# Half-row matmuls for the gates of a recurrent branch, two channel tiles to a group

## The chip, the cores and the metric

The kernel runs on one core of one Trainium2 chip. The time is device microseconds of one execution of the whole kernel. Besides plain timed runs there is one profiled execution, whose trace shows every engine's instructions: PE (TensorE's matmuls), PEld (its weight loads), DVE (VectorE), ACT (ScalarE), POOL (GpSimd) and SP (the engine that issues most DMAs). Data lies in a memory of 128 partitions; matmul results go to PSUM, which has eight banks of 128 partitions by 512 float32.

## The reference

One decoder block on 512 tokens of 1024 channels: a mixer with a pooling branch and a recurrent branch, then a gated convolutional FFN and a gated input embedding. The change is in the recurrent branch:

```python
xc = causal_dwconv(xb, conv_w, conv_b)                     # 512 tokens x 1024 channels
xh = xc.reshape(b, s, RNN_HEADS, RNN_HEAD_DIM)             # 16 heads of 64 channels
gates = jnp.einsum('bshi,ghij->gbshj', xh, w_gates)        # two gates, 64x64 weights per head
gates = gates.reshape(2, b, s, RNN_WIDTH) + b_gates[:, None, None, :]
r = sigmoid(gates[0]); i = sigmoid(gates[1])
log_a = -LRU_C * r * softplus(-lru_lambda)
u = sqrt(-expm1(2.0 * log_a)) * i * xc                     # 1 in place of the root at token 0
h = scan(h_t = exp(log_a_t) * h_{t-1} + u_t)
y_rnn = (h * gelu(gb)) @ w_rg_out
```

Each head's gate values depend on that head's 64 channels alone.

## The kernel before

Everything is kept with channels on partitions and the 512 tokens along the free dimension; 128 channels are a channel tile, and a channel tile of the recurrent branch holds two heads. Float32 products are made of three matmuls (`mm3`, L169 to L173): both operands are split into a high part, rounded to the type that TensorE takes at full rate (cast by ScalarE, `hi`), and the rest (subtracted by VectorE, `lo`), and high x high, high x low and low x high are summed in one bank.

The order on TensorE is the order in which the code is written; the other engines are ordered by a scheduler, with chains of their own for the sigmoids and other functions on ScalarE (`act`, L137) and for the recurrent branch's work on VectorE (`inv`). Weights are loaded by DMAs in SP's queue, split, and kept some tiles ahead in six buffers each.

The stage around the change is the loop `for n in range(12)` (L537). Four input tiles of the recurrent branch (`rx`) are made before it. Each step multiplies one more input tile (`in_tile(n)`, 24 matmuls), and for the branch's channel tiles goes through:

- `evac` (L454): VectorE scales the bank of an input tile into memory; tiles 8 and up of this count go to the GeLU gate's buffers `rg_t`.
- `conv_first`, `conv_rest`, `conv_low` (L472 to L487): the causal convolution, giving `xc`, and its high and low parts `xcs`, the gate matmuls' moving operand.
- `gates(c)`, at n = c + 4: six matmuls, three into each of two banks, one bank for gate r and one for gate i. The weights are block diagonal 128x128 tiles in `bdh` and `bdl`: head 2c's 64x64 block stands in the upper rows and left columns, head 2c+1's in the lower rows and right columns, and zeros (two POOL memsets, L397 and L398) elsewhere. Two sigmoids on ScalarE, 128 partitions each, follow.
- `gated(c)`, one step later (L503): VectorE multiplies gate i with `xc`.

After the loop `rnn_decay` (L505) makes the decay and runs the scan on VectorE, `rnn_out` multiplies with the GeLU gate, and `rnn_split` splits the result for the output product much later. Meanwhile TensorE goes on with the merge gates' and the pooling branch's input tiles (`IN_ORDER`); `pool_map` (from 170 us on) multiplies the pooled groups, which VectorE makes after the scan.

Of the kernel before, what the change touches and what calls it, by code (L numbers as in the profile page):

```python
# [8 lines left out]
F32 = mybir.dt.float32  # L9
F32R = mybir.dt.float32r  # L10
AF = mybir.ActivationFunctionType
ALU = mybir.AluOpType

P = 128
S = 512
D = 1024
KD = D // P
# [3 lines left out]
EPS = 1e-6  # L21
WINDOWS = (2, 4, 8, 16)
PAD = 16
AHEAD = 4
AHEAD0 = 2
LAG = 4
# [26 lines left out]
C_BG = 48  # L53
# [12 lines left out]
def block_kernel(  # L66
# [20 lines left out]
    nc = tc.nc  # L87
    ACT, V, PE = nc.scalar, nc.vector, nc.tensor

    const = ctx.enter_context(tc.tile_pool(name="const", bufs=1))  # L90
# [15 lines left out]
    def nm(s):  # L106
        uid[0] += 1
        return f"{s}{uid[0]}"

    def bank():  # L110
        return psum.tile([P, S], F32, tag="ps", name=nm("ps"))

    def temp(dt=F32, n=S):
        return tmp.tile([P, n], dt, tag="t", name=nm("t"))

    def slot(dt=F32):
        return mid.tile([P, S], dt, tag="m", name=nm("m"))

    def quad(tag, dt=F32R):
        return big.tile([P, 4, S], dt, tag=tag, name=nm(tag))  # L120
# [4 lines left out]
    def behind(ins, name):  # L125
        tc.add_manual_dep(
            ins.ins,
            name,
            mybir.DependencyInfo(mybir.DependencyClass.NoSync, mybir.DependencyReason.DATA),
            reason="order on the engine",  # L130
        )
# [3 lines left out]
    def act(o, i, func, after=None, **kw):  # L135

        ins = ACT.activation(o, i, func, **kw)  # L137
        after = after or last_func[0]
        if after is not None:
            behind(ins, after)  # L140
        last_func[0] = ins.ins.name
        return ins
# [3 lines left out]
    def inv(ins):  # L146

        if last_v[0] is not None:
            behind(ins, last_v[0])
        last_v[0] = ins.ins.name  # L150
        return ins
# [9 lines left out]
    def sub(o, a, b):  # L161
        V.tensor_tensor(o, a, b, ALU.subtract)  # L162

    def split(hi, lo, src):

        last_copy[0] = ACT.copy(hi, src)  # L166
        sub(lo, src, hi.bitcast(F32))

    def mm3(o, a, b, start, stop, **kw):  # L169
        (ah, al), (bh, bl) = a, b  # L170
        PE.matmul(o, ah, bh, start=start, stop=False, **kw)  # L171
        PE.matmul(o, ah, bl, start=False, stop=False, **kw)  # L172
        PE.matmul(o, al, bh, start=False, stop=stop, **kw)  # L173


    col = const.tile([P, C_END], F32, tag="col", name="col")
# [14 lines left out]
    def c1(j):  # L191
        return col[:, j : j + 1]
# [122 lines left out]

    def weight(key, ahead=AHEAD):
        i = order.index(key)
        while nxt[0] <= min(i + ahead, len(order) - 1):
            prep(order[nxt[0]])
            nxt[0] += 1  # L320
        return ready[key]
# [24 lines left out]
    def ht(k):  # L346
        return hth[k // 4][:, k % 4, :], htl[k // 4][:, k % 4, :]
# [3 lines left out]
    for k in range(KD):  # L351
        raw = xraw[k]
# [4 lines left out]
        hi, lo = ht(k)  # L357
        ht_done = ACT.activation(hi, raw, AF.Identity, scale=c1(C_GMIX + k)).ins.name
        V.scalar_tensor_tensor(lo, raw, c1(C_GMIX + k), hi.bitcast(F32), ALU.mult, ALU.subtract)
        if k % 2 == 1 and k < 7:  # L360
            if k > 1:
                xt = quad("C", F32)
                a = k // 2 - 1
# [23 lines left out]
    for k in range(KD):  # L387
        w = weight(("rx", k // 2), ahead=3)
        (wh, wl), (hh, hl) = w, ht(k)
        for i, (a, b) in enumerate(((wh, hh), (wl, hh), (wh, hl))):  # L390
            for m in range(4):
                o = (k % 2) * S + m * P
                PE.matmul(rx[m], a[:, o : o + P], b, start=k == 0 and i == 0, stop=k == KD - 1 and i == 2)  # L393


    bdh, bdl = quad("C"), quad("C")
    nc.gpsimd.memset(bdh.bitcast(F32), 0.0)  # L397
    nc.gpsimd.memset(bdl.bitcast(F32), 0.0)  # L398
    raw = wpool.tile([P, D], F32, tag="raw", name=nm("raw"), bufs=6)
    nc.sync.dma_start(raw, w_bd)  # L400
    H = P // 2
    for q in range(2):
        pr = slice(q * H, (q + 1) * H)
        hi, lo = (
            b.rearrange("p a (c j) -> p (a c) j", j=P)[pr, :, q * H : (q + 1) * H] for b in (bdh, bdl)
        )
        split(hi, lo, raw[pr].rearrange("p (c j) -> p c j", j=H))


    lam = col[:, C_LAM : C_LAM + 8]  # L410
# [1 line left out]
    mabs, e, f, s, s2, ncol, n2col = sp  # L412
# [31 lines left out]
    def in_tile(m):  # L444
        w = weight(("in", m), ahead=AHEAD if m > 6 else AHEAD0)
        ps = bank()
        for k in range(KD):
            mm3(ps, pick(w, k * P, (k + 1) * P), ht(k), k == 0, k == KD - 1)
            if m == 0 and k == 0:
                spread_rstd()  # L450
        return ps

    def scaled(ps, o):
        return V.tensor_tensor(o, ps, rb, ALU.mult)  # L454

    xs, xc, xcs, sig = {}, {}, {}, {}
    r_t, a_t, rg_t = {}, {}, {}
    rgq = [quad("C", F32), quad("C", F32)]

    def evac(n, ps):  # L460
        if n < 8:
            with urgent():
                xs[n] = temp()
                inv(scaled(ps, xs[n]))
        else:
            c = n - 8
            rg_t[c] = rgq[c // 4][:, c % 4, :]
            inv(scaled(ps, rg_t[c]))

    def conv_first(c):  # L470
        xc[c] = slot()
        ina(ACT.activation(xc[c], xs[c], AF.Identity, scale=c1(C_CONVW + 24 + c), bias=c1(C_CONVB + c)))  # L472

    def conv_rest(c):
        a = xc[c]
        for d in (1, 2, 3):
            inv(
                V.scalar_tensor_tensor(
                    a[:, d:], xs[c][:, : S - d], c1(C_CONVW + (3 - d) * 8 + c), a[:, d:], ALU.mult, ALU.add
                )  # L480
            )
        xcs[c] = slot(F32R), slot(F32R)
        ina(ACT.copy(xcs[c][0], a))

    def conv_low(c):
        hi, lo = xcs[c]
        inv(V.tensor_tensor(lo, xc[c], hi.bitcast(F32), ALU.subtract))  # L487

    def gates(c):
        pss = []  # L490
        for g in range(2):
            ps = bank()
            o = (c % 4) * P
            w = bdh[:, 2 * g + c // 4, o : o + P], bdl[:, 2 * g + c // 4, o : o + P]
            mm3(ps, w, xcs[c], True, True)
            pss.append(ps)
        r_t[c] = slot()
        act(r_t[c], pss[0], AF.Sigmoid, bias=c1(C_BG + c))
        sig[c] = temp()
        act(sig[c], pss[1], AF.Sigmoid, bias=c1(C_BG + 8 + c))  # L500

    def gated(c):
        inv(V.tensor_tensor(xc[c], sig[c], xc[c], ALU.mult))  # L503
# [33 lines left out]
    for n in range(12):  # L537
        banks.append(in_tile(n))
        if n == 0:
            for c in range(4):  # L540
                evac(c, banks[c])
            conv_first(0)
        if n < 8:
            if n < 7:
                if n + 1 in xs:
                    conv_first(n + 1)
            conv_rest(n)
        if 0 < n <= 8:
            conv_low(n - 1)
        if 0 <= n - LAG <= 7:  # L550
            gates(n - LAG)
        if 0 <= n - LAG - 1 <= 7:
            gated(n - LAG - 1)
        evac(4 + n, banks[4 + n])
        if n < 7 and n + 1 not in xc:
            conv_first(n + 1)
# [7 lines left out]
    def pool_tile(g):  # L564
        w = WINDOWS[g]
        ps = in_tile(12 + g)
        u = temp(n=S + PAD)
        V.memset(u[:, :PAD], 0.0)
        with tc.high_priority(offset=300):
            scaled(ps, u[:, PAD:])  # L570
        acc, d = u, 1
        while d < w:
            nx = temp(n=S + PAD)
            o = 2 * d if 2 * d < w else PAD
            V.tensor_tensor(nx[:, o:], acc[:, o:], acc[:, o - d : S + PAD - d], ALU.add)
            acc, d = nx, 2 * d
# [62 lines left out]
    for m in range(KD):  # L639
        w = weight(("wpo", m))  # L640
# [3 lines left out]
        w = weight(("wrg", m))  # L644
# [4 lines left out]
        a, b = gate[m], gate[8 + m]  # L649
# [4 lines left out]
        if m == PLE_AT:  # L654
            pled = dram.tile([S, D], F32, name="pled")
            pq = []
            for k in range(2):
                raw = temp()
# [8 lines left out]
    def token_major(name, nkp, lhs, tail=3):  # L667
# [10 lines left out]
        for t in range(NT):  # L678
            for kp in range(nkp - tail, nkp):
                for h in range(2):  # L680
                    w = weight((name, kp, h), ahead=AHEAD if t else 1)
                    for kk in range(2):
# [58 lines left out]
    def h2(b, c):  # L741

        return tuple(v[c][:, :, b * HALF : (b + 1) * HALF] for v in (h2h, h2l))

    def products(o, w, i, form, start):
        for k in range(4):
            lhs = tuple(v[:, i, k * P : (k + 1) * P] for v in w)
            rhs = tuple(v[:, k, :] for v in form)
            mm3(o, lhs, rhs, start and k == 0, k == 3, skip_group_check=True)

    def up_plain(f, b):
        for i in range(2):
            d = gb if f % 10 == 1 else ub
            if f < 20 and b == 0:
                d[i] = bank()
            w = weight(("up", 0, f), ahead=AHEAD - PLAIN.index(f) if b == 0 else AHEAD)
            products(d[i][:, b * HALF : (b + 1) * HALF], w, i, h2(b, f // 10 - 1), f < 20 and b == 0)
# [30 lines left out]
    for f in (5, 6, 7, 3):  # L788
        q = big.tile([P, 2, 4, HALF], F32R, tag="A", name=nm("A"))
# [141 lines left out]
    for t, i, pair in token_major("wd", 12, hid_split):  # L931
# [5 lines left out]
        with urgent():  # L937
            add_norm(pair, g_fpost, res)
            for h in range(2):
                n = slot()  # L940
# [7 lines left out]
    for h in range(2):  # L948
        for t in range(NT):
            i = 2 * (t % 2) + h  # L950
            o = temp()
            parts = ((0, S // 2), (S // 2, S)) if (h, t) == (1, NT - 1) else ((0, S),)
            for a, b in parts:
                ps = bank()
                for k in range(KD):
                    w = weight(("wpg", k // 2, h))
                    q = (k % 4) * P
# [85 lines left out]
```

## Time and profile before

| | |
|---|---|
| time, three runs | 769.15, 769.66, 769.69 us (median 769.66) |
| profiled execution | 769.33 us, its span 767.5 us |
| granted TensorE clock | 0.999 |
| PE busy | 761.7 us |
| DVE busy | 525.0 us |
| ACT busy | 395.1 us |
| gate matmuls | 48, the first at 56.4 us, the last at 105.1 us |
| sigmoids of the gates | 16 |

The span runs from the first to the last instruction; the profiled execution's own time is 1.8 us longer. In the timeline a row has its start, its length, the engine, the line of the kernel, the operation, the tile written and the tiles read, and the shape. A matmul's recorded length covers its passage through the array, so that records overlap: what one costs in a full stream is the distance from start to start. Of a waiting engine the trace says what ended its wait.

### The profile page before, as it was taken

The page shows a single profiled execution, that of the slowest core. Times are in us where ns is not written, and L with a number is a line of the kernel's source. Part 1 is how long each engine was busy: PE and PEld are TensorE (multiplying, and loading weights), DVE is VectorE, ACT ScalarE, POOL GpSimd, SP SyncE. Part 2 cuts the span into 40 slices and gives each one's busy share as a digit, 9 for nine tenths or more (in the row PEclk, how much of TensorE's full clock was granted, in tenths as well). Part 3 has the DMA queues.
Part 4 walks back from the last instruction along what each step waited for, and adds up shares of the span by engine and source line. Part 5 has one row for each costly group of instructions (what it writes and reads, how often), then busy time and mean ns, then how long its engine had stood idle before and what let it go on. Part 6 is the DMA issues. An engine that isn't in the chain of part 4 may idle for free.

```text
span 767.5 us, 11024 instructions
## 1 busy us (share of the span) xinstructions
PE 761.7 (99%) x4377; PEld 674.6 (88%) x4377; DVE 525.0 (68%) x710; ACT 395.1 (51%) x627; POOL 18.6 (2%) x29
## 2 busy tenths in 40 slices
PE   9999999999999999999999999999999999999997
PEld 7888888888888888889999999999999888888886
DVE  4898446998354655589998888889978332335852
ACT  6845369735232342277866666666685322224631
POOL 2000000000000000010000000000000000001100
PEclk9999999999999999999999999999999999999999
DMA  9752211233324449312233333333368323320111
GB/s 331 283 186 83 82 69 56 62 117 110 123 80 141 138 136 328 110 71 84 95 124 99 107 111 110 111 110 111 110 207 313 139 88 105 102 90 1 56 56 55
DMA packets 42004, 93.87 MB, mean 122 GB/s; under 512 B 3297, under 2 KB 3937, under 8 KB 41953
## 3 DMA queue, kind: packets, MB, share of 16 engines
q1 hardware_dynamic: 41808, 93.07, 35.9%
q8 instruction: 34, 0.56, 0.3%
q14 instruction: 18, 0.14, 0.1%
q10 hardware_dynamic: 144, 0.10, 0.0%
HBM read 86.87 MB, written 6.29 MB: 121 GB/s over the span
## 4 chain that ended last, share of the span: by engine, by line
PE 96%; DMA 2%; SPq 0%; DVE 0%; ACT 0%; POOL 0%; issue 0%; DVEq 0%
PE ps L171 32%; PE ps L172 32%; PE ps L173 32%; DMA C<-in_x_dram 1%; PE ps L700 1%; PE ps L393 1%; DMA col<-in_cols_dram 0%; ACT C L378 0%; SPq L356 0%; DVE lo L162 0%; POOL s L329 0%; PE ps L440 0%; SPq L364 0%; SPq L303 0%; DVE t L384 0%
## 5 line engine op out<-in xcount | busy, mean ns | idle before, releaser
L162 DVE TENSOR_TENSOR lo<-raw,hi 128x1024 fp32r<-128x1024 f32 (+2 forms) x167 | 193.4, 1178 | 88.0 <-ACT hi L311 66.7
L171 PE MATMUL ps<-A,hi 128*128 128x256 f32 (+1 forms) x608 | 199.5, 328 | 0.0
L173 PE MATMUL ps<-A,lo 128*128 128x256 f32 (+1 forms) x608 | 199.4, 328 | 0.0
L172 PE MATMUL ps<-A,hi 128*128 128x256 f32 (+1 forms) x608 | 199.4, 328 | 0.0
L311 ACT CAST hi<-raw 128x1024 fp32r<-128x1024 f32 (+1 forms) x94 | 94.1, 1008 | 154.2 <-PE ps L172 74.0
L173 PEld LDWEIGHTS ps<-A,lo 128*128 128x128 f32 x608 | 114.6, 188 | 10.1
L172 PEld LDWEIGHTS ps<-A,hi 128*128 128x128 f32 x608 | 114.6, 188 | 9.9
L171 PEld LDWEIGHTS ps<-A,hi 128*128 128x128 f32 x608 | 114.6, 188 | 9.9
L171 PE MATMUL ps<-C,hi 128*128 128x256 f32 (+1 forms) x392 | 118.0, 301 | 0.0
L172 PE MATMUL ps<-C,hi 128*128 128x256 f32 (+1 forms) x392 | 117.9, 301 | 0.0
L173 PE MATMUL ps<-C,lo 128*128 128x256 f32 (+1 forms) x392 | 117.8, 301 | 0.0
L171 PE MATMUL ps<-hi,A 128*128 128x512 f32 x256 | 100.0, 391 | 0.0
L173 PE MATMUL ps<-hi,A 128*128 128x512 f32 x256 | 99.7, 389 | 0.0
L172 PE MATMUL ps<-lo,A 128*128 128x512 f32 x256 | 99.7, 389 | 0.0
L166 ACT CAST hi<-raw 128x1024 fp32r<-128x1024 f32 x70 | 72.5, 1052 | 35.1 <-PE ps L172 24.6
L172 PEld LDWEIGHTS ps<-C,hi 128*128 128x128 f32 x392 | 74.2, 189 | 2.6
L171 PEld LDWEIGHTS ps<-C,hi 128*128 128x128 f32 x392 | 74.2, 189 | 2.5
L173 PEld LDWEIGHTS ps<-C,lo 128*128 128x128 f32 x392 | 74.2, 189 | 2.5
L173 PEld LDWEIGHTS ps<-hi,A 128*128 128x128 f32 x256 | 48.1, 188 | 10.0
L171 PEld LDWEIGHTS ps<-hi,A 128*128 128x128 f32 x256 | 48.1, 188 | 9.9
L172 PEld LDWEIGHTS ps<-lo,A 128*128 128x128 f32 x256 | 48.1, 188 | 9.7
L162 DVE TENSOR_TENSOR A<-m,A 128x512 fp32r<-128x512 f32 x40 | 26.0, 686 | 14.6 <-ACT A L166 14.2
(148 smaller groups left out, 918.5 us busy)
## 6 DMA issues: line engine op xcount, KB each, us to landing
raw<-in_w_up_dram SPq DMA_DIRECT2D x48, 512.0 KB, 3.4
raw<-in_w_in_dram SPq DMA_DIRECT2D x32, 512.0 KB, 3.8
raw<-in_w_down_dram SPq DMA_DIRECT2D x24, 512.0 KB, 3.4
raw<-in_w_rg_out_dram SPq DMA_DIRECT2D x8, 512.0 KB, 3.3
raw<-in_w_o_dram SPq DMA_DIRECT2D x8, 512.0 KB, 3.4
raw<-in_w_ple_gate_dram SPq DMA_DIRECT2D x8, 512.0 KB, 3.4
m<-in_rows_dram SPq DMA_DIRECT2D x10, 256.0 KB, 5.7
m<-in_x_t_dram SPq DMA_DIRECT2D x8, 256.0 KB, 7.3
```

The lines of the kernel that those rows point to most:

```text
L162: V.tensor_tensor(o, a, b, ALU.subtract)
L166: last_copy[0] = ACT.copy(hi, src)
L171: PE.matmul(o, ah, bh, start=start, stop=False, **kw)
L172: PE.matmul(o, ah, bl, start=False, stop=False, **kw)
L173: PE.matmul(o, al, bh, start=False, stop=stop, **kw)
L311: ACT.copy(hi, raw)
L393: PE.matmul(rx[m], a[:, o : o + P], b, start=k == 0 and i == 0, stop=k == KD - 1 and i == 2)
L700: PE.transpose(ps[:, q * P : (q + 1) * P], a[:, q * P : (q + 1) * P], ident)
```

## The change

The block diagonal tiles go. The gate weights now stand in one buffer `bd`: for channel tile c, 128 columns, of which the first 64 are gate r's weights and the last 64 gate i's, on rows 0 to 63 for head 2c and on rows 64 to 127 for head 2c+1, with the high parts in one half of the buffer and the low parts in the other. A gate matmul takes 64 rows of weights and 64 rows of `xcs` and writes 128 partitions of a bank of its own: partitions 0 to 63 are the head's gate r, 64 to 127 its gate i. The two heads of a channel tile use the two halves of TensorE's rows, in turn, and two banks.

Two channel tiles make a group of 12 matmuls with four banks: the groups stand behind input tiles 5, 7, 9 and 11, where before the six matmuls of one channel tile stood behind each of the input tiles 4 to 11. Since a bank now holds r and i of one head, four sigmoids of 64 partitions take the place of two of 128 for each channel tile; two of the four write to the other half of the partitions than they read, and take their bias from a small tile `bias` that two DMAs in SP's queue fill from the DRAM columns. The first channel tile's `gated` comes right behind its group, the second one's a step later. The two POOL memsets go, and one split of 128 partitions takes the place of two of 64.

```diff
-    bdh, bdl = quad("C"), quad("C")
-    nc.gpsimd.memset(bdh.bitcast(F32), 0.0)
-    nc.gpsimd.memset(bdl.bitcast(F32), 0.0)
+    bd = quad("C").rearrange("p (s a) c -> p s (a c)", s=2)
     raw = wpool.tile([P, D], F32, tag="raw", name=nm("raw"), bufs=6)
     nc.sync.dma_start(raw, w_bd)
-    H = P // 2
-    for q in range(2):
-        pr = slice(q * H, (q + 1) * H)
-        hi, lo = (
-            b.rearrange("p a (c j) -> p (a c) j", j=P)[pr, :, q * H : (q + 1) * H] for b in (bdh, bdl)
-        )
-        split(hi, lo, raw[pr].rearrange("p (c j) -> p c j", j=H))
+    split(
+        *(bd[:, i].rearrange("p (c g j) -> p g c j", g=2, j=HEAD) for i in range(2)),
+        raw.rearrange("p (g c j) -> p g c j", g=2, j=HEAD),
+    )
+    bias = const.tile([P, KD], F32, tag="bias", name="bias")
+    nc.sync.dma_start(bias[:HEAD], cols[HEAD:, C_BG : C_BG + KD])
+    nc.sync.dma_start(bias[HEAD:], cols[:HEAD, C_BG + KD : C_BG + 2 * KD])
...
-    def gates(c):
-        pss = []
-        for g in range(2):
-            ps = bank()
-            o = (c % 4) * P
-            w = bdh[:, 2 * g + c // 4, o : o + P], bdl[:, 2 * g + c // 4, o : o + P]
-            mm3(ps, w, xcs[c], True, True)
-            pss.append(ps)
-        r_t[c] = slot()
-        act(r_t[c], pss[0], AF.Sigmoid, bias=c1(C_BG + c))
-        sig[c] = temp()
-        act(sig[c], pss[1], AF.Sigmoid, bias=c1(C_BG + 8 + c))
+    def gates(cs):
+        pss = {}
+        for c in cs:
+            pss[c] = bank(), bank()
+            hi, lo = xcs[c]
+            o = slice(c * P, (c + 1) * P)
+            for i, (a, b) in enumerate(((0, hi), (0, lo), (1, hi))):
+                for ps, pr in zip(pss[c], HEADS):
+                    PE.matmul(ps, bd[pr, a, o], b[pr], start=i == 0, stop=i == 2)
+        ba, bb = HEADS
+        for c in cs:
+            r_t[c] = slot()
+            sig[c] = temp()
+            g = C_BG + c
+            act(r_t[c][ba], pss[c][0][ba], AF.Sigmoid, bias=col[ba, g : g + 1])
+            act(sig[c][ba], pss[c][0][bb], AF.Sigmoid, bias=bias[bb, c : c + 1])
+            act(r_t[c][bb], pss[c][1][ba], AF.Sigmoid, bias=bias[ba, c : c + 1])
+            act(sig[c][bb], pss[c][1][bb], AF.Sigmoid, bias=col[bb, g + KD : g + KD + 1])
...
-        if 0 <= n - LAG <= 7:
-            gates(n - LAG)
-        if 0 <= n - LAG - 1 <= 7:
+        if n > LAG and (n - LAG) % 2:
+            gates((n - LAG - 1, n - LAG))
+            gated(n - LAG - 1)
+        elif n > LAG:
             gated(n - LAG - 1)
```

`HEADS` are the row slices 0 to 63 and 64 to 127. The names and lines of the changed kernel stand some lines lower: `mm3` at L171 to L175, `act` at L139, the gate matmuls at L500.

More of the change, by code (lines that the diff above doesn't have):

```diff
@@ L23 @@
 PAD = 16
+HEAD = P // 2
+HEADS = slice(0, HEAD), slice(HEAD, P)
 AHEAD = 4
```

## The prediction

> **What bounds the kernel now.** I began with the page's busy shares and the chain of waits.
>
> ```profile
> span 767.5 us, 11024 instructions
> PE 761.7 (99%) x4377; PEld 674.6 (88%) x4377; DVE 525.0 (68%) x710; ACT 395.1 (51%) x627; POOL 18.6 (2%) x29
> ...
> PE 96%; DMA 2%; SPq 0%; DVE 0%; ACT 0%; POOL 0%; issue 0%; DVEq 0%
> ```
>
> TensorE is busy for 761.7 of 767.5 us and makes up 96% of the chain. Only a stage table tells whether that holds where the gates are, so I cut the span at the first and after the last gate matmul (stages 56.30 to 105.30) and at the first pool map (170). The columns are the length, then PE, PEld, DVE, ACT and POOL busy, the granted clock, the DMA share and GB/s.
>
> ```profile
> 56.30:105.30 49.00, 49.00 (x217) 40.57 (x217) 29.61 (x40) 22.28 (x31) 0.00 (x0) 1.00 0.24 80
> 105.30:170.00 64.70, 64.70 (x287) 53.59 (x286) 53.42 (x85) 49.56 (x73) 0.00 (x0) 1.00 0.24 82
> 170.00:220.00 50.00, 50.00 (x222) 41.40 (x221) 28.26 (x42) 19.14 (x29) 0.00 (x0) 1.00 0.30 95
> ```
>
> In the gate stage PE fills 49.00 of 49.00 us at full clock, with DVE at 29.6 and ACT at 22.3. The two stages behind it are full as well. So a microsecond taken from the gate matmuls reaches the end, as long as nothing PE reads later comes too late. The gate matmuls themselves, by tile and then in time (start, length):
>
> ```profile
> L171 PE MATMUL ps<-m,C x16: 389/389/390, 56.4 to 104.6; 128*128 128x512 f32 x16
> ...
> L173 PE MATMUL ps<-m,C x16: 389/389/390, 56.8 to 105.1; 128*128 128x512 f32 x16
> ```
>
> ```profile
> 103.95 0.39 PE L171 MATMUL ps<-m,C 128*128 128x512 f32 x1
> 104.18 0.39 PE L172 MATMUL ps<-m,C 128*128 128x512 f32 x1
> ...
> 105.08 0.39 PE L173 MATMUL ps<-m,C 128*128 128x512 f32 x1
> 105.31 0.39 PE L171 MATMUL ps<-A,hi 128*128 128x512 f32 x1
> ```
>
> There are 48 (three lines of 16, of which two are shown). A record is 0.39 us long, but starts follow each other in (105.31 - 103.95) / 6 = 0.227 us: that is what one costs, and 0.39 - 0.227 = 0.163 us is the tail that the next one covers. The gates take 48 x 0.227 = 10.88 us of PE, half of it multiplying zeros.
>
> **The change, part by part.** *The matmuls.* Still 48, each now on 64 rows, issued in 24 pairs whose members use different halves of the rows and different banks. No row of this trace has a half-row matmul, so a pair lies between 0.227 us (both stream together) and 0.454 us (one after the other). What supplies them can be read: the spacing of weight loads at their closest, and matmuls half as wide.
>
> ```profile
> 29.69 0.19 PEld L171 LDWEIGHTS ps<-A,hi 128*128 128x128 f32 x1
> 29.80 0.19 PEld L172 LDWEIGHTS ps<-A,hi 128*128 128x128 f32 x1
> ```
>
> ```profile
> 400.05 0.28 PE L171 MATMUL ps<-C,hi 128*128 128x256 f32 x1
> 400.17 0.29 PE L172 MATMUL ps<-C,hi 128*128 128x256 f32 x1
> ```
>
> Loads follow each other in 0.11 us, and with 256 columns a load and a matmul go through every 0.12 us. Two loads of 128 columns thus need 0.22 to 0.24 us, about one stream of 512 columns. I take 0.227 for a pair, since the two members share neither rows nor banks, and keep 0.240 as the bound if loads set the pace. 24 pairs are 5.44 us (to 5.76).
>
> *The switches.* Each of four groups of 12 is entered from full-row work and left to it: 8 switches. The nearest row is the change to the plain fp32 matmuls of L440 and back.
>
> ```profile
> 28.68 0.39 PE L173 MATMUL ps<-A,lo 128*128 128x512 f32 x1
> 28.91 1.05 PE L440 MATMUL ps<-t,ones 128*128 128x128 f32 x8
> 29.72 0.47 PE L171 MATMUL ps<-A,hi 128*128 128x512 f32 x1
> 30.03 0.39 PE L172 MATMUL ps<-A,hi 128*128 128x512 f32 x1
> ```
>
> Going in costs nothing (0.23 from 28.68 to 28.91); coming back, the first matmul takes 0.31 instead of 0.227, or 0.08 more. That is the low end for a switch. The high end is a full drain with a load behind it: 0.163 + 0.188 = 0.35. I take the drained tail alone, 0.163, between the two: 8 x 0.163 = 1.30 us (0.6 to 2.8). [...]
>
> *The offset in a group.* The second half's first weights come behind the first half's, so a group ends one load later, 0.19 us: 4 x 0.19 = 0.75 us (0.11 each, 0.44, by the closest loads).
>
> Sum on PE: 5.44 + 1.30 + 0.75 = 7.49 us against 10.88, **3.39 us less**. The ends are 5.44 + 0.64 + 0.44 = 6.5 (4.4 less) and 5.76 + 2.80 + 0.75 = 9.3 (1.6 less); with switches free, too, 5.0 to 5.4 less.
>
> How the groups now stand on TensorE. Before, behind input tile 4 (ps_538), the gates of channel tile 0: L171 to L173, two banks, weights in C_306 and C_307.
>
> ```order
> L172 MATMUL ps_538<-A_107,hi_450 128x512
> L173 MATMUL ps_538<-A_105,lo_451 128x512
> L171 MATMUL ps_572<-m_401,C_306 128x512
> L172 MATMUL ps_572<-m_402,C_306 128x512
> L173 MATMUL ps_572<-m_401,C_307 128x512
> L171 MATMUL ps_576<-m_401,C_306 128x512
> L172 MATMUL ps_576<-m_402,C_306 128x512
> L173 MATMUL ps_576<-m_401,C_307 128x512
> ```
>
> Now, one input tile later (ps_577 is tile 5), the first group; left out are each channel tile's last pairs, which differ from those shown in the weights' columns or operand alone:
>
> ```order
> L174 MATMUL ps_577<-A_107,hi_490 128x512
> L175 MATMUL ps_577<-A_105,lo_491 128x512
> L500 MATMUL ps_611<-m_399,C_306 128x512
> L500 MATMUL ps_612<-m_399,C_306 128x512
> L500 MATMUL ps_611<-m_400,C_306 128x512
> L500 MATMUL ps_612<-m_400,C_306 128x512
> ...
> L500 MATMUL ps_619<-m_440,C_306 128x512
> L500 MATMUL ps_620<-m_440,C_306 128x512
> ...
> L173 MATMUL ps_647<-A_104,hi_532 128x512
> ```
>
> Neighbours differ in bank and in row half. Tile 0's gates come one input tile later, and tile 1's where they were, so no operand is later for them than before.
>
> *ScalarE and what hangs on it.* The sigmoids double in number, not in length: an instruction covers 64 partitions but the same 512 columns. Their cost, and the start of the decay behind the last ones:
>
> ```profile
> 77.68 0.68 ACT L137 ACTIVATE m<-ps,col 128x512 f32<-128x512 f32 x1
> 78.31 0.69 ACT L137 ACTIVATE t<-ps,col 128x512 f32<-128x512 f32 x1
> ...
> 104.88 0.68 ACT L137 ACTIVATE m<-ps,col 128x512 f32<-128x512 f32 x1
> 105.51 0.69 ACT L137 ACTIVATE t<-ps,col 128x512 f32<-128x512 f32 x1
> 106.22 1.28 ACT L137 ACT_TABLE_LOAD   x1
> ```
>
> From start to start 0.63 us; 16 more are 10 us on an ACT with 27 us free in this stage. A group has eight in a row, 5.0 us. Before, the last channel tile's two stood so:
>
> ```order
> L311 CAST hi_1091<-raw_1089 128x1024
> L137 ACTIVATE m_932<-ps_924,col 128x512
> L137 ACTIVATE t_934<-ps_928,col 128x512
> L137 ACT_TABLE_LOAD
> L137 ACTIVATE m_939<-m_580,sp_321 128x512
> ```
>
> Now:
>
> ```order
> L313 CAST hi_1105<-raw_1103 128x1024
> L139 ACTIVATE m_938<-ps_922,col 64x512
> L139 ACTIVATE t_939<-ps_922,bias 64x512
> L139 ACTIVATE m_938<-ps_923,bias 64x512
> L139 ACTIVATE t_939<-ps_923,col 64x512
> L139 ACTIVATE m_944<-ps_930,col 64x512
> L139 ACTIVATE t_945<-ps_930,bias 64x512
> L139 ACTIVATE m_944<-ps_931,bias 64x512
> L139 ACTIVATE t_945<-ps_931,col 64x512
> L139 ACT_TABLE_LOAD
> ```
>
> Eight sigmoids, not two, stand between the last gate matmuls and the decay. Their times: a group of my sum is 7.49 / 4 = 1.87 us, so the last one starts at 103.95 - 7 x 1.36 + 3 x 1.87 = 100.0, its first bank is done near 101.2, and eight sigmoids end near 106.2, where the decay's table load stands today. PE is 3.4 us ahead by then, so whatever hangs on this chain loses 3.4 us of lead. The tightest such lead is that of the first pool map (ps<-m,hi), whose input DVE finishes behind the scan:
>
> ```profile
> 162.75 0.69 DVE L162 TENSOR_TENSOR m<-t,m 128x512 fp32r<-128x512 f32 x1
> ```
>
> ```profile
> 170.59 0.39 PE L171 MATMUL ps<-m,hi 128*128 128x512 f32 x1
> ```
>
> 7.1 us of lead now, 3.7 after; about 1 us less if DVE's order, which has one more weight split (1.2 us) ahead of this row, does not make it up. If the cover went, PE would wait here for the shortfall alone. Behind the sigmoids DVE's product with xc (L503, now waiting for the fourth sigmoid, 4 to 5 us after an input tile's end) holds up the eviction of that tile, L454. Its bank is wanted three input tiles on, over 12 us later; the second to fourth bank of a group wait for sigmoids one to five or six of the group before, over 5 us earlier.
>
> *The rest* is hidden. Two 64x8 DMAs go into SP's queue behind w_bd, one split replaces two, and two POOL memsets go.
>
> ```profile
> 15.45 0.33 SPq L400 DMA_DIRECT2D raw<-in_w_bd_dram  x1
> 18.00 5.86 SPq L303 DMA_DIRECT2D raw<-in_w_in_dram  x2
> ```
>
> ```profile
> 29.71 2.46 DVE L162 TENSOR_TENSOR C<-raw,C 64x1024 fp32r<-64x1024 f32 x2
> ```
>
> ```profile
> 2.99 1.80 POOL L398 MEMSET C<- 128x2048 f32 x1
> 20.43 1.03 POOL L329 TENSOR_TENSOR s<-s,mhalf 128x4 f32<-128x4 f32 x1 [15.64 <-DVE s L380]
> ```
>
> The DMAs hold back input tiles 3 and 4 by two issues, some 0.7 us; those are multiplied from about 46 us on (the first gates, at 56.4, follow tile 4, and a tile is 5.4 us), 20 us later. The split saves DVE 1.2 us under a busy PE, and POOL idled 15.6 us behind its memsets.
>
> **The rivals.** *The halves do not overlap*, so the change does not do what it says: 48 x 0.227 stays, and the switches come on top, 8 x 0.163 = 1.3 us, **771.0** (0.08 to 0.35 each: 770.3 to 772.5). For it: every matmul shown starts a full stream after the one before. Against it: those all share rows. With my switches and offsets the change loses from 0.368 us a pair on, (10.88 - 2.05) / 24.
>
> *A half's next weights wait for its own stream.* Then a pair is 0.227 + 0.11 to 0.188 = 0.337 to 0.415 us, 24 of them 8.1 to 10.0, with 2.05 of switches and offsets 10.1 to 12.0: **769.0 to 770.8**, middle 769.9. Against it, loads now run under a stream on the same rows:
>
> ```profile
> 56.35 0.19 PEld L172 LDWEIGHTS ps<-m,C 128*128 128x128 f32 x1
> ```
>
> ```profile
> 56.35 0.39 PE L171 MATMUL ps<-m,C 128*128 128x512 f32 x1
> ```
>
> Both start at 56.35, on all 128 rows. [...]
>
> *The lead of the pool map goes* and PE waits there: up to 2 us given back, 768.3.
>
> **How the numbers follow.** The profiled execution took 769.33 us, 1.8 around its span; less 3.39 that is 765.9. The median of the runs is 0.33 higher, so I forecast **766.3**, with 764.3 to 768.1 as this case's own range (5.4 to 1.6 less). Chances: forecast 0.68; no overlap 0.17; own-stream weights 0.12; lost lead 0.03. A measurement of this kernel can tell about 0.2%, 1.54 us, from no change. Faster by more: 0.68. Slower by more: 0.12 of the first rival and 0.04 of the second, 0.16. Within: 0.16. The range reaches from 764.4 into the first rival, to 770.4.
>
> **What would show it.** Each group of gate matmuls (L500) is about 1.9 us from its first start to the next full-row matmul, instead of 2.72; members of a pair start under 0.2 us apart, pairs 0.227 to 0.24. The first matmul of a group and the first behind it start about 0.16 us late. The decay's table load stands near 106, the first pool map near 167 with no PE idle before it. Starts 0.227 us apart within a group would prove the first rival, pairs 0.34 us or more apart the second, idle time before the pool map the third. A group over 2.72 us makes the forecast wrong.

## The result, and the profile after

The changed kernel takes 765.29 us (median of 4 runs, 765.22 to 766.04) against 769.48 us (769.15 to 769.69) for the kernel before on the same chip: a ratio of 0.9948, with a 95% interval of 0.9931 to 0.9965. That is faster by more than the 0.2% that can be told. The forecast was 766.3 us with 764.3 to 768.1 as its own range; the gain is 4.2 us where 3.4 were worked out.

The page of the changed kernel, the lines that answer to those shown of before: span, busy time by engine, chain of waits by engine.

```profile
span 763.4 us, 11051 instructions
PE 758.2 (99%) x4377; PEld 669.6 (88%) x4377; DVE 524.0 (69%) x709; ACT 406.3 (53%) x642; POOL 15.2 (2%) x27
...
PE 96%; DMA 2%; DVE 0%; ACT 0%; SPq 0%; POOL 0%; issue 0%; DVEq 0%
```

The span is 4.1 us shorter and PE's busy time 3.5 us. The number of PE instructions is the same, 4377, and so is PE's share of the chain. The time went out of TensorE's own work. The stage table of the changed kernel (same columns as before) is cut at the start of its last full-row matmul before the first group, and then from behind the last group to just ahead of the first pool map:

```profile
61.30:101.50 40.20, 40.20 (x195) 31.21 (x194) 23.00 (x30) 28.22 (x38) 0.00 (x0) 1.00 0.23 79
101.50:166.00 64.50, 64.50 (x285) 53.38 (x285) 50.58 (x79) 50.84 (x75) 0.00 (x0) 1.00 0.24 80
```

PE is still full at full clock there and behind it, so nothing given up by the gates is lost to a wait. What the gates cost is read from the timeline of the changed kernel's PE around the first group (start, length; the row of L500 puts its 12 matmuls together):

```profile
61.30 0.39 PE L175 MATMUL ps<-A,lo 128*128 128x512 f32 x1
61.62 1.66 PE L500 MATMUL ps<-m,C 64*128 64x512 f32 x12
63.21 0.50 PE L173 MATMUL ps<-A,hi 128*128 128x512 f32 x1
63.55 0.40 PE L174 MATMUL ps<-A,hi 128*128 128x512 f32 x1
```

Here and below I price a group as the time from the start of the last full-row matmul before it (61.30) to the start of the second one behind it (63.55), less the two full-row matmuls in that stretch at 0.227 us each. This way both switches are inside. It gives 63.55 - 61.30 - 0.454 = 1.80 us, where the kernel before paid 12 x 0.227 = 2.72. The forecast had 1.87.

How the 1.80 us are made up, from the same timeline cut into windows that hold one pair each:

```profile
61.62 0.50 PE L500 MATMUL ps<-m,C 64*128 64x512 f32 x2
61.96 0.40 PE L500 MATMUL ps<-m,C 64*128 64x512 f32 x2
62.19 0.40 PE L500 MATMUL ps<-m,C 64*128 64x512 f32 x2
```

and of the weight loads (PEld), the loads of the first two pairs:

```profile
61.62 0.19 PEld L500 LDWEIGHTS ps<-m,C 64*128 64x128 f32 x2 [0.35 <-issue]
61.73 0.19 PEld L500 LDWEIGHTS ps<-m,C 64*128 64x128 f32 x2
```

Two matmuls on different halves lie within the same 0.50 us and their two loads within the same 0.19 us: members of a pair start together, and so do their loads. From the second pair on, pairs follow in 62.19 - 61.96 = 0.23 us. Entering costs 61.62 - 61.30 = 0.32 us instead of 0.227, 0.09 more; what the group waits for there is not shown. The first pair's loads begin with it, not a stream ahead of it (PEld stood idle for 0.35 us before), its record is 0.50 us long where the next one's is 0.40, and the second pair follows it in 61.96 - 61.62 = 0.34, 0.11 more than the pace. Leaving does much the same: the first full-row matmul comes some 0.1 late, its record is 0.50 us long, and 63.21 to 63.55 is 0.34. So a switch costs 0.09 + 0.11 = 0.20 us, and a group 6 x 0.23 + 2 x 0.20 = 1.8 us. Groups of other lengths, below, bear out both numbers.

For the whole stage I take a point before the first gates that both programs pass with the same work done, the last matmul of input tile 4, and one behind the last gates, the second full-row matmul. Before:

```profile
56.12 0.39 PE L173 MATMUL ps<-A,lo 128*128 128x512 f32 x1
...
105.54 0.39 PE L172 MATMUL ps<-A,hi 128*128 128x512 f32 x1
```

After:

```profile
55.86 0.39 PE L175 MATMUL ps<-A,lo 128*128 128x512 f32 x1
...
101.61 0.40 PE L174 MATMUL ps<-A,hi 128*128 128x512 f32 x1
```

The stretch takes 49.42 us before and 45.75 after: 3.67 us less, which is 4 x (2.72 - 1.80) = 3.7. The other 0.4 us of the 4.1 between the spans lie outside the gates: 0.26 because PE came to the stage that much earlier, and the rest behind it. The experiments below show that the arrival at this stage differs by about 1 us from profile to profile, so I claim no cause for that 0.26. (In the profile of the kernel before, PE waits 0.3 and 0.2 us ahead of the stage, in the matmuls of L393, for VectorE and ScalarE; in the changed kernel's it doesn't, but in some of the runs below it does.)

### The profile page after: what moved, and what is told of

Same layout as the page of the kernel before. It is cut to its first block, busy times and chain, and to the rows that moved or that the text cites. A ratio compares the mean times of both kernels' runs of the same rounds, so it can differ in the third digit from the quotient of the medians.

```text
span 763.4 us, 11051 instructions
## 1 busy us (share of the span) xinstructions
PE 758.2 (99%) x4377; PEld 669.6 (88%) x4377; DVE 524.0 (69%) x709; ACT 406.3 (53%) x642; POOL 15.2 (2%) x27
## 4 chain that ended last, share of the span: by engine, by line
PE 96%; DMA 2%; DVE 0%; ACT 0%; SPq 0%; POOL 0%; issue 0%; DVEq 0%
PE ps L173 31%; PE ps L174 31%; PE ps L175 31%; DMA C<-in_x_dram 1%; PE ps L710 1%; PE ps L500 1%; PE ps L395 1%; DMA m<-in_x_t_dram 1%; ACT C L380 0%; SPq L303 0%; DVE lo L164 0%; POOL s L331 0%; PE ps L442 0%; DVE t L386 0%; ACT t L139 0%
## 5 line engine op out<-in xcount | busy, mean ns | idle before, releaser
L175 PE MATMUL ps<-A,lo 128*128 128x256 f32 (+1 forms) x608 | 199.3, 328 | 0.0
L175 PEld LDWEIGHTS ps<-A,lo 128*128 128x128 f32 x608 | 114.5, 188 | 10.1
L175 PE MATMUL ps<-C,lo 128*128 128x256 f32 (+1 forms) x392 | 117.8, 300 | 0.0
L175 PE MATMUL ps<-hi,A 128*128 128x512 f32 x256 | 99.6, 389 | 0.0
L175 PEld LDWEIGHTS ps<-C,lo 128*128 128x128 f32 x392 | 74.2, 189 | 2.5
L175 PEld LDWEIGHTS ps<-hi,A 128*128 128x128 f32 x256 | 48.1, 188 | 10.0
```

## The experiments

Each group price below is worked out as above. Ratios are to the kernel before on the same chip, beside the same runs: 769.48 us (27 runs) for the first four experiments, 769.90 (7 runs) for the half columns and the three groups, 769.44 (15 runs) for the one half and the two repeats.

### Do two halves have to stand next to each other?

The first kernel issues, for each group, the six matmuls of the first half of the rows, and then the six of the second.

```diff
-        for c in cs: ... for ps, pr in zip(pss[c], HEADS):
-            PE.matmul(ps, bd[pr, a, o], b[pr], ...)
+        for q, pr in enumerate(HEADS):
+            for c in cs: ...
+                PE.matmul(pss[c][q], bd[pr, a, o], b[pr], ...)
```

> The changed kernel with another order inside each group of 12: first the six matmuls on rows 0 to 63, then the six on rows 64 to 127. Theory A (the gain comes from two half-row streams running side by side): only the sixth and seventh can share a stream, so a group is 11 streams of 0.234 us and 0.41 us of switches, 2.98 us instead of the 1.81 us that the changed kernel's trace shows; four groups add 4.7 us: 770.0 us, slower than the kernel before by about 0.5 us. Rival B (a matmul on 64 rows is cheap by itself): the same 765.3 us as the changed kernel.

It took 767.89 us (ratio 0.9978, 0.9969 to 0.9988), between the two. The first group in its PE timeline:

```profile
61.33 0.39 PE L175 MATMUL ps<-A,lo 128*128 128x512 f32 x1
61.65 2.23 PE L501 MATMUL ps<-m,C 64*128 64x512 f32 x12
63.81 0.50 PE L173 MATMUL ps<-A,hi 128*128 128x512 f32 x1
64.15 0.40 PE L174 MATMUL ps<-A,hi 128*128 128x512 f32 x1
```

A group costs 64.15 - 61.33 - 0.454 = 2.37 us, not the 1.80 of the changed kernel and not the 2.98 of one half after the other. To see where the overlap lies, that kernel's stage view of line L501 alone, in slices of one stream (length, then PE busy and how many of the group's matmuls lie in the slice, PEld the same, clock, DMA):

```profile
61.63:61.86 0.23, 0.21 (x1) 0.21 (x2) 1.00 0.00 0
61.86:62.09 0.23, 0.23 (x2) 0.19 (x2) 1.00 0.00 0
62.09:62.32 0.23, 0.23 (x4) 0.18 (x3) 1.00 0.00 0
...
63.47:63.70 0.23, 0.23 (x2) 0.00 (x0) 1.00 0.00 0
```

One matmul is there at first, two in the second slice (a record is longer than a slice), and four from the third on. The twelve starts fit two chains of six, each with the group's own pattern (0.34 us, then 0.23), the second chain beginning at 62.23, 0.58 us behind the first. The records don't name the rows, so that the second chain is the second half of the rows is inferred from this spacing. The run on one half, below, strengthens it: there matmuls on the same rows start 0.231 us apart on average, while here the first of the second chain starts within 0.01 us of the third of the first. It would mean that matmuls of the second half started while earlier ones of the first half still waited, ahead of the program's order. Neither theory had that: neighbours needn't alternate for the halves to overlap, but the overlap then begins about 2.5 streams late, and each group loses 0.57 us.

### Is the switch as dear as it looks?

Eight groups of one channel tile instead of four of two: the pairs stay, the switches double.

```diff
-        if n > LAG and (n - LAG) % 2:
-            gates((n - LAG - 1, n - LAG))
+        if 0 <= n - LAG <= 7:
+            gates((n - LAG,))
```

> The changed kernel with one channel tile to a group: eight groups of six half-row matmuls behind the input tiles 4 to 11. Theory A (a group pays 0.41 us for entering and leaving, whatever its length): eight groups of 3 x 0.234 + 0.41 = 1.11 us are 8.9 us against 7.2: 1.6 us more, 766.9 us. Rival B (the extra over the streams belongs to the pairs, not to the switch): 765.3 us. Rival C (a switch drains the array for 0.35 us each way, as the prediction's high end has it): 768 us.

It took 767.19 us (0.9971, 0.9959 to 0.9983), the median 0.3 above what was expected. Its second group on PE, the one behind input tile 5, where the changed kernel's first one stands (the group behind tile 4 costs the same 1.10):

```profile
62.74 0.39 PE L175 MATMUL ps<-A,lo 128*128 128x512 f32 x1
63.06 0.96 PE L500 MATMUL ps<-m,C 64*128 64x512 f32 x6
...
64.29 0.40 PE L174 MATMUL ps<-A,hi 128*128 128x512 f32 x1
```

64.29 - 62.74 - 0.454 = 1.10 us for three pairs. Against the 1.80 of six pairs that makes (1.80 - 1.10) / 3 = 0.233 us a pair and 1.10 - 3 x 0.233 = 0.40 for entering and leaving, 0.20 for each switch. Grouping two channel tiles saves 8 x 1.10 - 4 x 1.80 = 1.6 us of PE.

### What the grouping and the doubled sigmoids do alone

The kernel before, with groups of two channel tiles and each sigmoid cut into two of 64 partitions, but the gates' matmuls on all rows.

```diff
+            for g, ps in enumerate(pss[c]):
+                mm3(ps, w, xcs[c], True, True)
...
+            for pr in (slice(0, P // 2), slice(P // 2, P)):
+                act(r_t[c][pr], pss[c][0][pr], AF.Sigmoid, ...)
```

> The kernel before with two parts of the change alone: two channel tiles to a group at the changed kernel's places, and four sigmoids of 64 partitions to a channel tile; the matmuls keep all 128 rows and the zeros. Theory A (half rows are the whole gain; grouping and doubled sigmoids are hidden): 769.5 us, within 0.2% of before, gate matmuls 10.88 us of PE. Rival B (grouping alone gains or the sigmoids alone cost): off by 1 us or more.

It took 769.34 us (1.0, 0.999 to 1.001): no difference. Its busy line:

```profile
PE 761.7 (99%) x4377; PEld 674.4 (88%) x4377; DVE 525.1 (68%) x710; ACT 405.6 (53%) x643; POOL 18.7 (2%) x29
```

ACT works 10.5 us more than in the kernel before (405.6 against 395.1) and PE exactly as long, 761.7. The sixteen added sigmoids are hidden, and the grouping alone is worth nothing on full rows. What is left for the gain in this stage is the halves.

### What if the lead of the pool map goes?

The last group's eight sigmoids are done twice; the result of the first pass is overwritten with the same values.

```diff
+            for _ in range(2 if c > 5 else 1):
                 act(r_t[c][ba], pss[c][0][ba], AF.Sigmoid, ...)
                 ... (the four of a channel tile)
```

> The changed kernel with the last group's eight sigmoids done twice (same values), 5.6 us more on ScalarE ahead of the decay. Theory A (the first pool map hangs on this chain with a lead of 1.8 us in the changed kernel's trace): PE waits 5.6 - 1.8 = 3.8 us before that map, and 769.1 us in all; if VectorE makes up part of it, 767 to 769. Rival B (this chain has more lead than the trace suggests): 765.3 us and no PE idle there.

It took 768.84 us (0.9992, 0.9982 to 1.0001); its ten times lie between 767.31 and 769.89. The PE timeline of the profiled execution:

```profile
167.07 0.39 PE L175 MATMUL ps<-A,lo 128*128 128x512 f32 x1
168.25 0.50 PE L173 MATMUL ps<-m,hi 128*128 128x512 f32 x1 [0.78 <-ACT m L168]
169.54 0.50 PE L174 MATMUL ps<-m,hi 128*128 128x512 f32 x1 [0.79 <-DVE m L164]
...
170.12 0.39 PE L173 MATMUL ps<-A,hi 128*128 128x512 f32 x1
...
173.33 0.63 PE L173 MATMUL ps<-A,hi 128*128 128x512 f32 x1
173.75 0.63 PE L174 MATMUL ps<-A,hi 128*128 128x512 f32 x1
```

PE waits twice at the first pool map: first for the split's first half on ACT, then for the rest on DVE, the chain that the prediction named. From 167.07 to the fourth matmul behind it, at 170.12, PE takes 3.05 us where four matmuls take 4 x 0.227 = 0.91 in the changed kernel: 2.1 us lost. But it doesn't end there. Stages of the same kernel:

```profile
167.00:170.00 3.00, 1.42 (x6) 0.64 (x5) 2.97 (x6) 1.57 (x2) 0.00 (x0) 1.00 0.77 257
170.84:174.25 3.41, 3.41 (x10) 2.63 (x9) 3.33 (x9) 1.53 (x2) 0.00 (x0) 0.50 0.57 199
174.25:176.00 1.75, 1.75 (x9) 1.45 (x8) 1.75 (x3) 0.66 (x2) 0.00 (x0) 1.00 0.00 0
```

The column behind the counts is the granted clock: 1.00 in a stage in which PE worked only 1.42 of 3 us, then 0.50 for 3.41 us, from 170.84 on, and 1.00 again. Matmuls start up to 0.42 us apart there (173.33 to 173.75) instead of 0.227. By 174.92, 18 matmuls behind the one at 167.07, 7.85 us have gone where the changed kernel takes 18 x 0.227 = 4.1: 3.8 us lost in all, 1.6 of them by the clock. In this execution the forecast for a lost lead, "PE would wait here for the shortfall alone", is too low by almost half. That the loss equals the 3.8 us expected of this run is chance: the waits cost only 2.1 of it and the clock the rest. VectorE had the operand 4.6 us later than in the changed kernel, not 5.6, and PE itself came 0.6 us later to this point.

The ten times stand in two groups of five, 767.3 to 768.4 and 769.3 to 769.9, and their granted clocks go with them: 0.999 or 1.0 in each of the first five, 0.997 or 0.998 in each of the others. A clock of 0.5 for 3.41 us takes 0.2% off the mean of 768 us, so the drop fits the second group and is missing in the first. Without it the median is 768.05, 2.8 us above the changed kernel's 765.29; with it 769.43, 4.1 above. What decides between the two isn't shown. That the waits brought the drop is read from their order in time; what speaks for it is that in the profiled executions of all other kernels here the mean granted clock is 0.999 or 1.0, and in those of the kernel before and the changed kernel it stays at 1.00 from 8 to 761 us. The drop came behind two gaps of 0.8 us each, within 2.5 us.

### Do weight loads of the two halves go one at a time?

Each gate matmul is cut into two of 256 columns. The streamed columns stay the same, and the loads and matmuls double to 24 a group.

```diff
+            for h in (slice(0, HALF), slice(HALF, S)):
                 for i, (a, b) in enumerate(...):
-                        PE.matmul(ps, bd[pr, a, o], b[pr], ...)
+                        PE.matmul(ps[:, h], bd[pr, a, o], b[pr, h], ...)
```

> The changed kernel with each gate matmul cut into two of 256 columns: 96 half-row matmuls and 96 weight loads in 48 pairs. Theory A (the two halves' weight loads run side by side, as their starts 3 ns apart in the changed kernel's trace suggest): a pair of 256 columns every 0.12 us as for a single full-row matmul of that width, 48 pairs 5.8 us instead of 5.6: 765.5 us. Rival B (loads of 128 columns pass one at a time, 0.11 us apart, as the prediction had it): 0.22 us a pair, 10.6 us: 770 us.

It took 765.52 us (0.9951, 0.9934 to 0.9967), as the changed kernel. Its first group:

```profile
61.15 0.39 PE L175 MATMUL ps<-A,lo 128*128 128x512 f32 x1
61.47 1.69 PE L501 MATMUL ps<-m,C 64*128 64x256 f32 x24
...
63.42 0.40 PE L174 MATMUL ps<-A,hi 128*128 128x512 f32 x1
```

63.42 - 61.15 - 0.454 = 1.82 us with 24 loads. One load behind the other, at the closest spacing of 0.11 us, they alone would take 24 x 0.11 = 2.6. So the loads of the two halves run side by side, and there is no load that the second half has to wait for.

### Is it the overlap, or are half-row matmuls cheap?

All twelve matmuls of a group on the first half of the rows. The gates of the upper heads are left out (their banks get products of the lower heads instead).

```diff
-                for ps, pr in zip(pss[c], HEADS):
-                    PE.matmul(ps, bd[pr, a, o], b[pr], ...)
+                for ps in pss[c]:
+                    PE.matmul(ps, bd[HEADS[0], a, o], b[HEADS[0]], ...)
```

> The changed kernel with all 12 matmuls of a group on rows 0 to 63: both heads' banks are made from the lower head's 64 rows of weights and channels, so the upper heads' own gates are left out. Theory A (two halves side by side are the gain): a group is 12 streams of 0.234 us and 0.41 us of switches, 3.22 us instead of 1.81; four groups add 5.6 us: 770.9 us, slower than the kernel before by 1.4 us, and no two starts are nearer than 0.22 us. Rival B (a matmul on 64 rows is cheap by itself, which the run with the halves apart left open, since it took 2.3 us less than 12 and 2.1 less than 11 streams a group would): 765.3 to 768 us.

It took 771.35 us (1.0022, 1.0013 to 1.0031), slower than the kernel before. Its first group:

```profile
62.06 0.39 PE L175 MATMUL ps<-A,lo 128*128 128x512 f32 x1
62.38 3.03 PE L500 MATMUL ps<-m,C 64*128 64x512 f32 x12
65.35 0.50 PE L173 MATMUL ps<-A,hi 128*128 128x512 f32 x1
```

From 62.06 to 65.35 are 3.29 us, where the changed kernel has 63.21 - 61.30 = 1.91: 1.38 more, or six streams of 0.23. A matmul on half the rows takes about as long as one on all of them, and the gain is the overlap alone. From the group's second matmul (62.72) to its last (65.03), ten steps, starts are 0.231 us apart on average, against 0.227 on all rows. This run is also the price of the first rival, measured: 771.35 against the 771.0 forecast for it. (By the sums of the expectation, 12 streams a group are 770.9 us, so the run with the halves apart took 3.0 us less than that, not 2.3.)

### Larger groups

Groups of three, three and two channel tiles, behind input tiles 6, 9 and 11.

```diff
-        if n > LAG and (n - LAG) % 2:
-            gates((n - LAG - 1, n - LAG))
+        n_groups = {6: (0, 1, 2), 9: (3, 4, 5), 11: (6, 7)}
+        if n in n_groups:
+            gates(n_groups[n])
```

> The changed kernel with groups of three, three and two channel tiles behind input tiles 6, 9 and 11 (six, six and four banks at once), and each input tile's eviction ahead of the group's products. Theory A (a group pays 0.41 us for its two switches): one group less, 0.4 us less, 764.9 us, which only the trace can tell from the changed kernel. Rival B (six banks at once hold up the input tiles): PE waits before the input tile behind a group, and the time is above 765.3 us.

It took 764.98 us (0.9942, 0.9927 to 0.9957). Its first group:

```profile
66.86 0.39 PE L175 MATMUL ps<-A,lo 128*128 128x512 f32 x1
67.18 2.35 PE L500 MATMUL ps<-m,C 64*128 64x512 f32 x18
...
69.80 0.40 PE L174 MATMUL ps<-A,hi 128*128 128x512 f32 x1
```

69.80 - 66.86 - 0.454 = 2.49 us for nine pairs. With the 1.10 of three pairs that is (2.49 - 1.10) / 6 = 0.232 us a pair, and 0.40 for the two switches. Three groups instead of four should save one entry and one exit, 0.4 us. To see whether that shows in the time, both kernels were run once more together.

> The changed kernel once more, on the same chip as the one with three channel tiles to a group: 765.3 us. Where the start of its span differs from the kernel before, by up to 1 us either way as between the runs so far, the gate stage alone still differs by 3.6 us.

> Groups of three, three and two channel tiles once more. If a group costs 0.41 us for its switches, 0.4 us below the changed kernel on the same chip, 764.9 us; if the 0.3 us between the first two runs were scatter, the same time.

The changed kernel took 765.57 us (0.9952, 0.9938 to 0.9965), the one with three groups 765.42 (0.9948, 0.9935 to 0.996): no difference that can be told. In the trace the gate stage of the latter is 0.4 us shorter, but in this pair of profiled executions it loses more than that ahead of the stage, where PE waits for one of ACT's copies (the waits of the kernel with three groups: the engine and line that wait, what for, us in total, times, longest):

```profile
PE ps L395 <- ACT A L360: 0.8, 1, 0.8
```

Lines L395 and L360 are not touched by the change. The changed kernel's second profile takes the same 45.75 us from the last matmul of tile 4 to the second one behind the gates as the first did, though it enters that stretch at 55.19 us instead of 55.86. So the stage repeats to a hundredth, and the way to it varies by more than one group less would save.

## Why the prediction was right, and where its sizes were off

**What bounds the kernel.** Right. PE stays full in the gate stage and behind it, and the run with the gates on full rows (ACT 10.5 us longer, time the same) shows that the engines beside it don't count there. They do count once a lead is used up, as the run with doubled sigmoids shows.

**The pair.** 0.232 us measured; 0.227 taken, with 0.240 as the bound. The bound was argued from loads that set the pace; the cut into 256 columns shows that they don't. The 0.005 is not the price of pairing: on one half of the rows, without pairs, starts are 0.231 us apart. Why half rows take that much longer stays open. 24 pairs are 5.6 us, 0.1 over the 5.44 of the sum. In the changed kernel's trace the first pair's members start 3 ns apart, both inside 0.50 us.

**The switches.** 0.163 each taken, 0.20 measured, 1.6 us in place of 1.30. I took the drained tail alone; what happens is a smaller delay of 0.09 us, whose cause stays open, and then 0.11 more behind the first matmul. The second part goes with the first pair's loads, which begin with the pair instead of ahead of it. It is not the second pair's loads that are late: in the run with 256 columns the second pair's loads begin 0.11 us ahead of their matmuls (the row of x4 begins with the second pair),

```profile
61.58 0.19 PEld L501 LDWEIGHTS ps<-m,C 64*128 64x128 f32 x2
```

```profile
61.69 0.40 PE L501 MATMUL ps<-m,C 64*128 64x256 f32 x4
```

and in the changed kernel 0.23 ahead (61.73 and 61.96). The return from the fp32 matmuls of L440, the row I took for the low end, shows this second part alone: its load begins 0.03 us ahead (29.69 and 29.72), its record is 0.47 long instead of 0.39, and 0.08 is lost. The high end, 0.35, is refuted by the groups of one tile. That TensorE drains at a switch, as my 0.163 supposed, no run shows: there is a delay on the way in, but at 0.09 us it is less than the 0.163 of a full stream's tail.

**The offset in a group.** This is the step that failed: "The second half's first weights come behind the first half's, so a group ends one load later, 0.19 us". Loads of the two halves start together and run side by side, so there is nothing to be late by. 0.75 us fall out of the sum.

Together the measured terms are 5.6 + 1.6 + 0 = 7.2 us against 7.49, 3.7 less than the 10.88 before instead of 3.39. The sum is as near as this partly by luck: pairs and switches were taken 0.4 too low, the offset 0.75 too high. The forecast was 1.0 us too high: 0.3 by these terms, 0.4 by what lies outside the gates, and 0.3 by my adding the distance from the profiled execution to the median, which the runs of the changed kernel don't have (765.22 profiled, 765.29 median).

**ScalarE and the lead of the pool map.** The chain was read rightly, its sizes were not. The ACT timeline of the changed kernel:

```profile
104.93 0.68 ACT L139 ACTIVATE m<-ps,bias 64x512 f32<-64x512 f32 x1
105.63 0.69 ACT L139 ACTIVATE t<-ps,col 64x512 f32<-64x512 f32 x1
106.33 1.28 ACT L139 ACT_TABLE_LOAD   x1
```

The table load stands at 106.33 (106.2 forecast), and a sigmoid on 64 partitions is as long as one on 128 (0.68 and 0.69 us), but the sigmoids start every 0.70 us, not every 0.63; that the last group came earlier made up for it. And the lead is smaller than either 3.7 or 2.7 us. DVE and PE at the first pool map, and the row of the kernel before that answers to the second addition of L585:

```profile
161.74 1.43 DVE L585 TENSOR_TENSOR t<-t 128x526 f32<-128x526 f32 x2
163.09 1.22 DVE L164 TENSOR_TENSOR lo<-raw,hi 128x1024 fp32r<-128x1024 f32 x1
164.22 0.68 DVE L164 TENSOR_TENSOR m<-t,m 128x512 fp32r<-128x512 f32 x1
```

```profile
166.69 0.39 PE L173 MATMUL ps<-m,hi 128*128 128x512 f32 x1
```

```profile
163.97 0.68 DVE L575 TENSOR_TENSOR t<-t 128x512 f32<-128x512 f32 x1
```

The operand is done at 164.22 + 0.68 = 164.90 and wanted at 166.69: 1.8 us. PE is 3.9 us earlier than before, 0.5 more than forecast, and DVE 1.5 later. The weight split ahead of the operand (163.09, 1.2 us) was not made up, as the prediction's lower figure feared, and one of the pooling branch's additions, some 0.6 us, now stands ahead of it, too; before, it came behind (163.97). The doubled sigmoids did not hold this chain up: the table load behind them is only 0.1 us later than before, and VectorE's split of the recurrent branch's result begins at 151.99, 0.24 us earlier than before. The cover held, with 1.8 us left of 7.1. What lies behind it is steeper than forecast: with it gone, the run with doubled sigmoids lost 2.8 us, and 4.1 where the clock dropped, not up to 2.

**The rivals.** No overlap: refuted by the starts within a pair, and priced by the run on one half. A half's next weights wait for its own stream: refuted by the pace of 0.232 us a pair, and by the load at 61.73, which runs while both halves of the rows stream (61.62 to 62.12). The lost lead did not come.

## What to carry to other kernels

Where TensorE bounds the stage, two matmuls with a contraction of 64 are worth putting side by side on the two halves of the rows: a pair saved 0.22 us of 0.454, and each group paid about 0.40 us for entering and leaving. By that sum a group gains from two pairs on (three were the fewest that ran), and what counts is the number of groups. Put members of a pair next to each other in the program: with the halves apart, a group took 0.57 us more. When the engine that bounds a kernel gets faster, look up the leads of what it reads later: here 3.9 us less on PE and 1.5 us more work ahead of the operand on VectorE ate 5.3 of 7.1 us of lead. When 5.6 us more went into that chain, PE's waits cost 2.1 us in the profiled execution, and the clock behind them 1.6 more.

## What the runs showed of the hardware that was not expected

- Loads of 64 rows for the two halves start together and run side by side: 24 loads and 24 matmuls of 256 columns in a group of 1.82 us.
- Six matmuls of one half issued ahead of six of the other still overlap, 0.58 us late; from the spacing, TensorE starts matmuls ahead of earlier ones in the program when they use the other half. That the order is left is inferred, not read from a record.
- A switch between full-row and half-row work cost 0.20 us in each direction, in groups of 6, 12 and 18 matmuls alike.
- Two waits of 0.8 us each on PE were followed by a granted clock of 0.5 for 3.4 us, which cost 1.6 us; in five of ten executions the mean clock was 0.997 or 0.998, in the others 0.999 or 1.0.
- Sigmoids of 512 columns from a bank, from start to start: 0.58 to 0.63 us on 128 partitions (61.47, 62.06; 104.88, 105.51 in the kernel before); on 64 partitions 0.70 in the changed kernel, but 0.58 and 0.69 in turn in the run on full rows (104.57, 105.15, 105.84, 106.43). In both runs the longer steps are those to a sigmoid that reads the other half of the partitions than the one before it. That this is the cause is not shown.
